# Second half of a hybrid attention and hyena layer on one core: low parts of three projections on VectorE, the first merge chunk by token halves, the loads of the second modulation from GpSimd's queue

## The chip, the cores and the metric

The kernel runs on one core of one Trainium2 chip. The metric is the device time of one launch in microseconds. The core's engines are TensorE (PE: matrix products and transposes), VectorE (DVE), ScalarE (ACT), GpSimd (POOL) and SyncE (SP). Each of them works its instructions off in their order. A DMA is started by the engine in whose order its issue stands; before the change nearly all of them stand on SP. TensorE's clock is granted at one of two levels, 1.2 and 2.4 GHz, and the profile shows the granted share of the full one.

## What is computed

One layer over 1024 tokens of width 1024: two token mixers side by side, attention (8 heads) and a hyena long convolution (512 channels), each projected to the model's width, gated, added, and passed through one output projection with a gated residual. A norm with a second modulation and a feed-forward net follow. What bears on the change:

```python
m = silu(c) @ w_mod + b_mod                     # six modulation vectors of 1024
# modulation 2, 3 and 4, 5: the second half, "w_mod2" in the kernel
y  = sigmoid(g_attn) * (attn @ w_attn_out) + sigmoid(g_hyena) * (hyena @ w_hyena_out)
x  = x + gate1 * (y @ w_o + b_o)
h2 = rmsnorm(x, norm2) * (1 + scale2) + shift2  # then the feed-forward net
```

All is float32. The kernel splits each float32 operand of a product into a high part (`hi`, rounded to the shorter float32r) and a low part (`lo` = operand minus `hi`) and adds three products, hi*hi, hi*lo and lo*hi (`mm3`, lines L184 to L186).

## The kernel before

Stages follow one another: attention, then the hyena merge, the attention-branch merge, the output projection `wo`, the feed-forward net. A scheduler puts the instructions of these stages into one fixed order for each engine; tiles come from pools with a fixed number of buffers, and an instruction that needs a buffer waits until its last reader is done.

**Weights.** A block of weights is loaded by SP (`raw`), rounded by ScalarE (`whi`), and the low part `wlo` is made by one subtraction of 128 x 512 (`sub`, L174). `load_w` does this for the merges, `halves_of` for the output projection. In this part of the program that subtraction runs on GpSimd (`G`), except for the first hyena chunk, which has it on VectorE.

**Hyena merge** (L1242 on). The hyena output is stored by tokens and turned by TensorE into `hyh` and `hyl` (high and low part), four z tiles of which two make up each half of 512 tokens; a z tile gives two channel blocks, each by four transposes into a PSUM tile `tr` (2 buffers), a cast on ScalarE and a subtraction on VectorE. All four z tiles come first in the program, then four chunks `ci` of two output blocks `m2`. `branch` computes one output block over both token halves into a PSUM tile `mm` (3 buffers): per half 4 k steps of three matmuls. The result is multiplied by the sigmoid of `sg` (loaded by SP, sigmoid on ScalarE) and stored as `th_d`. In all 192 matmuls of 512 columns.

**Attention-branch merge** (L1262 on). The same with 8 k steps, on the attention output `oTh`, `oTl`; to its product the stored `th` is added, and the sum is split into `m0h`, `m0l` (first token half) and `m1h`, `m1l`. 384 matmuls. The last piece of the attention output is made by GpSimd (`ou`, `oTl`) and ScalarE (`oTh`).

**Output projection** (`wo_part`, `wo_get`). Four parts (token half, column half), each of 8 k steps over 4 row tiles, 384 matmuls in all. `wo_get` keeps five blocks of `w_o` loaded and three split ahead. At the end of a part VectorE evacuates each PSUM tile: `tm` (times the gate row), `Yt` plus `tm`, and in the first column half `Yt` plus the bias row `brow`. Beside the second token half, the first half is normed and turned (`first_rows`, `first_tile`: transposes L1391, `hf`, `m0h`, `m0l`); for odd blocks the low part `m0l` is on GpSimd.

**The second modulation** (`mod2`) runs beside all three stages, one step of four loads at each `background(1)`: for each of 8 blocks (j, n), 8 loads of 256 KB of `w_mod2` into `wm` (3 buffers), each multiplied by its part of silu(c) and added into `acc` by VectorE (L1209, L180). When four loads of the next block are done, `row_out` adds up `acc` over the partitions (high part `ah` on ScalarE, low part `al` on VectorE, two matmuls with a column of ones into `tr`), loads the row of `b_mod2`, adds it on VectorE (`row`), and stores the row in `m2_d`. All these transfers are SP's (`ld` is SP's issue of a DMA).

The functions that the change touches, with what calls them:

Of the kernel before, what the change touches and what calls it, by code (L numbers as in the profile page):

```python
# [15 lines left out]
P = 128  # L16
# [149 lines left out]
def build(tc, A, out, stop=99):  # L166
# [1018 lines left out]
    def row_out():  # L1185
# [9 lines left out]
        row = mp.tile([1, 512], F32, name="row", tag="row", bufs=2)  # L1195
        ld(out=row, in_=A["b_mod2"][j:j + 1, 512 * n:512 * n + 512])
        tt(row, row, ps[0:1], ALU.add)
        ld(out=m2_d[j:j + 1, 512 * n:512 * n + 512], in_=row)

    def mod2():  # L1200

        for j in (2, 0, 1, 3):
            for n in range(2):
                acc = mp.tile([P, 512], F32, name="acc", tag="acc", bufs=2)
                for k in range(KT):
                    raw = mp.tile([P, 512], F32, name="wm", tag="wm", bufs=3)
                    ld(out=raw, in_=A["w_mod2"][j, k][:, 512 * n:512 * n + 512])
                    if k == 0:
# [13 lines left out]
    hyl = [z.tile([P, 4, 512], F32R, name="hyl") for z in (zp_, zp2)]  # L1222
    for j, (half, a4) in enumerate(ZT):
        zt = zts[j] if j < 3 else z_load(half, a4)
        for c2 in range(2):
            c = 2 * half + c2
            tp = ptr.tile([P, 512], F32, name="tr", tag="tr")
            for a in range(4):
                T.transpose(tp[:, a * P:a * P + P], zt[:, a, c2 * P:c2 * P + P], ident)
            S.copy(out=hyh[a4][:, c], in_=tp)  # L1230
            sub(hyl[a4][:, c], tp, hyh[a4][:, c])

    def branch(w, m2, kt, rh, rl):
        ps = pmm.tile([P, L], F32, name="mm", tag="mm")
        for h in range(2):
            cs = slice(512 * h, 512 * h + 512)
# [6 lines left out]
    for ci in range(4):  # L1243
        w = load_w(A["w_hy"][ci], wp, G, nraw=5) if ci else load_w([raw_hy[:, 0], raw_hy[:, 1]], wp, V, nraw=5)
        for m2 in range(2):
            m = 2 * ci + m2
            ps = branch(w, m2, 4, hyh, hyl)
            sg = sgp.tile([P, L], F32, name="sg", tag="sg")
# [13 lines left out]
    for ci in range(4):  # L1262
        w = load_w(A["w_attn"][ci], wp, G, nraw=5)
        for m2 in range(2):
# [64 lines left out]
    def wo_get(half, n, k):  # L1329
# [4 lines left out]
        for b_ in wo_blocks[i:i + 3]:  # L1334
            if b_ not in wo_ready:
                wo_ready[b_] = halves_of(wo_raw_[b_], G)
        return wo_ready[half, n, k]
# [71 lines left out]
    def first_tile(c):  # L1409
        h2_tile(0, c, ptr.tile([P, 512], F32, name="tr", tag="tr"), hf0[:, c], S if c % 2 else V)  # L1410
        to_parts([b_[:, c] for b_ in B1], hf0[:, c], G if c % 2 else V)

# [462 lines left out]
```

## Time and profile before

| | |
|---|---|
| time, median of 3 runs | 1963.72 us (1960.64 to 1965.02) |
| profiled execution | 1968.5 us, span 1966.8 us |
| mean granted clock of TensorE | 0.979 |
| TensorE, VectorE busy | 1883.7 us (96%), 1548.1 us (79%) |
| ScalarE, GpSimd busy | 968.0 us (49%), 200.6 us (10%) |
| hyena merge | 1051.0 to 1103.5 us |
| attention-branch merge | 1103.5 to 1193.2 us |
| output projection | 1193.2 to 1297.6 us |
| DMA queues | SP 287.01 MB, ScalarE 33.76 MB, GpSimd none |

A program orders the rows by engine: "busy" is the time in which an engine executes, "idle before" the time in which it stood before an instruction, with the instruction or DMA that released it. The times are those of one profiled execution, counted from its span's start; the span is 1.7 us shorter than the time of that execution.

### The profile page before, as it was taken

The numbers are of one execution on the slowest core, as the hardware profiler recorded it, in microseconds if no ns is written. First come the engines' busy times: TensorE is split into PE (matmuls) and PEld (weight loads), VectorE is DVE, ScalarE is ACT, GpSimd is POOL, SyncE is SP. The second block draws the span as 40 slices with busy tenths as digits, with TensorE's granted clock in tenths as the row PEclk, the third lists the DMA queues.
The fourth block names the chain that finished last, engine by engine and source line by source line (L and its number), as shares of the span: only waits on it lengthen the run. The fifth ranks groups of instructions, "written<-read, shape, count | busy, mean of one in ns | idle before, by whom it ended". The sixth has DMA issues, their size and how long they took to land.

```text
span 1966.8 us, 27637 instructions
## 1 busy us (share of the span) xinstructions
PE 1883.7 (96%) x9776; PEld 1567.7 (80%) x9776; DVE 1548.1 (79%) x2753; ACT 968.0 (49%) x1958; POOL 200.6 (10%) x147
## 2 busy tenths in 40 slices
PE   7899999999999999999998999999999999899997
PEld 1788788999898987888887787778888888678885
DVE  6999996895978764777776555988888888878787
ACT  3855553432534365777775232454444444445443
POOL 0000000000000002445412233510000000000000
PEclk8999999999999999999999999999999999999998
DMA  8517437756554433544408865632323333358762
GB/s 297 181 57 249 133 135 237 220 177 196 185 169 148 156 136 102 151 136 143 145 17 216 297 215 209 214 113 86 118 97 123 102 113 107 124 182 320 252 204 96
DMA packets 181130, 322.53 MB, mean 164 GB/s; under 512 B 26955, under 2 KB 65359, under 8 KB 180096
## 3 DMA queue, kind: packets, MB, share of 16 engines
q1 hardware_dynamic: 156256, 287.01, 44.8%
q10 hardware_dynamic: 24736, 33.76, 4.8%
q8 instruction: 77, 1.26, 0.3%
q14 instruction: 61, 0.50, 0.1%
HBM read 245.03 MB, written 75.68 MB: 163 GB/s over the span
## 4 chain that ended last, share of the span: by engine, by line
PE 64%; DVE 19%; issue 5%; DMA 4%; ACT 3%; POOL 0%; SPq 0%; ACTq 0%; DVEq 0%; POOLq 0%
PE mm L184 8%; PE mm L185 8%; PE mm L186 8%; PE b L184 5%; PE b L186 5%; PE b L185 5%; PE tp L1145 3%; DVE ua L180 2%; DVE ug L180 2%; PE s L184 2%; PE s L186 2%; PE s L185 2%; PE o L185 2%; PE o L186 2%; PE o L184 2%
## 5 line engine op out<-in xcount | busy, mean ns | idle before, releaser
L184 PE MATMUL mm<-hTh,whi 128*128 128x512 f32 x448 | 177.8, 397 | 3.1 <-ACT sg L974 1.4
L185 PE MATMUL mm<-hTl,whi 128*128 128x512 f32 x448 | 177.1, 396 | 0.0
L186 PE MATMUL mm<-hTh,wlo 128*128 128x512 f32 x448 | 176.0, 393 | 0.0
L1047 DVE TENSOR_REDUCE mx<-s 128x1 f32<-128x512 f32 (+1 forms) x192 | 113.4, 598 | 55.3 <-PE s L186 53.6
L174 DVE TENSOR_TENSOR wlo<-raw,whi 128x512 fp32r<-128x512 f32 x158 | 106.6, 688 | 45.4 <-ACT whi L1513 32.1
L1052 ACT ACTIVATE Pt<-s,mx 128x512 f32<-128x512 f32 (+1 forms) x192 | 116.2, 616 | 18.4 <-DVE mx L1050 17.0
L184 PE MATMUL mm<-whi,hTh 128*128 128x256 f32 x416 | 119.6, 289 | 4.2 <-ACT whi L497 3.2
L174 DVE TENSOR_TENSOR PTl<-tp,PTh 128x512 fp32r<-128x512 f32 x160 | 108.4, 685 | 14.7 <-ACT PTh L1147 11.2
L185 PE MATMUL mm<-wlo,hTh 128*128 128x256 f32 x416 | 119.8, 289 | 0.0
L186 PE MATMUL mm<-whi,hTl 128*128 128x256 f32 x416 | 119.6, 288 | 0.0
L1147 ACT CAST PTh<-tp 128x512 fp32r<-128x512 f32 x160 | 92.9, 594 | 40.5 <-PE tp L1145 40.5
L186 PE MATMUL b<-bh,al 128*128 128x512 f32 x284 | 110.6, 389 | 0.6 <-DVE al L174 0.6
L184 PE MATMUL b<-bh,ah 128*128 128x512 f32 x284 | 110.6, 389 | 0.3 <-ACT ah L1732 0.3
L185 PE MATMUL b<-bl,ah 128*128 128x512 f32 x284 | 110.6, 389 | 0.0
L497 ACT CAST whi<-raw 128x512 fp32r<-128x512 f32 x110 | 67.1, 618 | 79.6 <-PE mm L185 37.7
L388 ACT CAST Xh<-X 128x512 fp32r<-128x512 f32 x128 | 77.8, 620 | 51.5 <-DVE X L177 18.9
L184 PEld LDWEIGHTS mm<-hTh,whi 128*128 128x128 f32 x448 | 84.7, 189 | 19.2 <-ACT sg L974 1.8
L174 DVE TENSOR_TENSOR Xl<-X,Xh 128x512 fp32r<-128x512 f32 x128 | 85.1, 682 | 18.1 <-ACT Xh L388 17.6
L174 POOL TENSOR_TENSOR qT<-qf,qT 128x1024 fp32r<-128x1024 f32 x7 | 16.7, 2393 | 801.5 <-ACT qT L1019 801.5
L186 PEld LDWEIGHTS mm<-hTh,wlo 128*128 128x128 f32 x448 | 84.5, 189 | 15.5 <-DVE wlo L174 0.2
L174 POOL TENSOR_TENSOR wlo<-raw,whi 128x512 fp32r<-128x512 f32 x54 | 80.0, 1493 | 161.6 <-ACT whi L497 103.1
L1145 PEld LDWEIGHTS tp<-ident,Pt 128*128 128x128 f32 x640 | 78.0, 141 | 22.7 <-issue 3.8
(385 smaller groups left out, 5761.1 us busy)
## 6 DMA issues: line engine op xcount, KB each, us to landing
raw<-w_up SPq DMA_DIRECT2D x132, 256.0 KB, 2.8
raw<-w_in SPq DMA_DIRECT2D x88, 256.0 KB, 4.3
wm<-w_mod SPq DMA_DIRECT2D x64, 256.0 KB, 4.2
raw<-act_d SPq DMA_DIRECT2D x25, 512.0 KB, 3.2
wd<-w_down SPq DMA_DIRECT2D x44, 256.0 KB, 3.6
ws_d<-wd SPq DMA_DIRECT2D x44, 256.0 KB, 4.4
act_d<-ug SPq DMA_DIRECT2D x44, 256.0 KB, 2.2
ft<-fwd_d SPq DMA_DIRECT2D x28, 384.0 KB, 3.7
```

The source lines that it names most:

```text
L174: eng.tensor_tensor(out=out, in0=a, in1=b, op=ALU.subtract)
L180: eng.scalar_tensor_tensor(out=out, in0=a, scalar=s, in1=b, op0=op0, op1=op1)
L184: T.matmul(o, lh, rh, start=start, stop=False, skip_group_check=more)
L185: T.matmul(o, lh, rl, start=False, stop=False, skip_group_check=more)
L186: last_mm[0] = T.matmul(o, ll, rh, start=False, stop=stop, skip_group_check=more)
L388: S.copy(out=h, in_=X)
L497: S.copy(out=hi, in_=raw)
L1047: V.tensor_reduce(out=mx[:, j:j + 1], in_=s[:, :n], axis=AX.X, op=ALU.max)
L1052: S.activation(out=Pt[:, o:o + n], in_=sps[j][:, :n], func=AF.Exp, bias=mx[:, 3:4], accum_out=sm[:, j:j + 1])
L1145: T.transpose(tp[:, i * P:i * P + P], cur[i][:, kt * P:kt * P + P], ident)
L1147: S.copy(out=th, in_=tp)
```

## The change

Three edits, all between the end of attention and the end of the output projection. First, the low parts of the hyena weights of chunks 1 to 3 (6 subtractions), of the attention-branch weights (16) and of `w_o` (32), and the four odd `m0l` of `first_tile`, move from GpSimd to VectorE. Second, the z tiles become a function: the first chunk of the hyena merge transposes the two z tiles of the first token half, multiplies that half for both output blocks, then transposes the other two z tiles and multiplies the second half into the same PSUM tiles. Third, the loads of `wm`, of the `b_mod2` rows and the stores of `m2_d` are issued from GpSimd's queue (`G.dma_start`) instead of SP's. GpSimd has no other work left in these stages after its last `ou` and `oTl`.

```diff
@@ row_out, mod2
-        ld(out=row, in_=A["b_mod2"][j:j + 1, 512 * n:512 * n + 512])
+        G.dma_start(out=row, in_=A["b_mod2"][j:j + 1, 512 * n:512 * n + 512])
         tt(row, row, ps[0:1], ALU.add)
-        ld(out=m2_d[j:j + 1, 512 * n:512 * n + 512], in_=row)
+        G.dma_start(out=m2_d[j:j + 1, 512 * n:512 * n + 512], in_=row)
...
-                    ld(out=raw, in_=A["w_mod2"][j, k][:, 512 * n:512 * n + 512])
+                    G.dma_start(out=raw, in_=A["w_mod2"][j, k][:, 512 * n:512 * n + 512])
@@ hyena merge
-    for j, (half, a4) in enumerate(ZT):
+    def z_tile(j):
+        half, a4 = ZT[j]
...
-    def branch(w, m2, kt, rh, rl):
-        ps = pmm.tile([P, L], F32, name="mm", tag="mm")
-        for h in range(2):
+    def branch(w, m2, kt, rh, rl, hs=(0, 1), ps=None):
+        ps = pmm.tile([P, L], F32, name="mm", tag="mm") if ps is None else ps
+        for h in hs:
...
-        w = load_w(A["w_hy"][ci], wp, G, nraw=5) if ci else load_w([raw_hy[:, 0], raw_hy[:, 1]], wp, V, nraw=5)
+        w = load_w(A["w_hy"][ci], wp, nraw=5) if ci else load_w([raw_hy[:, 0], raw_hy[:, 1]], wp, nraw=5)
+        if ci == 0:
+            z_tile(0)
+            z_tile(1)
+            first = [branch(w, m2, 4, hyh, hyl, (0,)) for m2 in range(2)]
+            z_tile(2)
+            z_tile(3)
         for m2 in range(2):
...
-            ps = branch(w, m2, 4, hyh, hyl)
+            ps = branch(w, m2, 4, hyh, hyl, (1,), first[m2]) if ci == 0 else branch(w, m2, 4, hyh, hyl)
@@ attention-branch merge
-        w = load_w(A["w_attn"][ci], wp, G, nraw=5)
+        w = load_w(A["w_attn"][ci], wp, nraw=5)
@@ output projection, first_tile
-                wo_ready[b_] = halves_of(wo_raw_[b_], G)
+                wo_ready[b_] = halves_of(wo_raw_[b_])
...
-        to_parts([b_[:, c] for b_ in B1], hf0[:, c], G if c % 2 else V)
+        to_parts([b_[:, c] for b_ in B1], hf0[:, c])
```

What the scheduler makes of it is shown at three places, all in VectorE's order. The first is the start of the hyena merge: `hyl` of `hyh0` is of the first token half, of `hyh1` of the second; `acc` is an accumulation of the second modulation. Before:

```order
L174 TENSOR_TENSOR hyl_12221<-tr_12244,hyh0_12219 128x512
L174 TENSOR_TENSOR hyl_12222<-tr_12251,hyh1_12220 128x512
L1209 TENSOR_SCALAR acc_12319<-wm_12320,sc_178 128x512
L174 TENSOR_TENSOR hyl_12222<-tr_12258,hyh1_12220 128x512
L174 TENSOR_TENSOR hyl_12222<-tr_12267,hyh1_12220 128x512
L180 SCALAR_TENSOR_TENSOR acc_12319<-wm_12323,sc_178,acc_12319 128x512
```

After:

```order
L174 TENSOR_TENSOR hyl_12221<-tr_12252,hyh0_12219 128x512
L1209 TENSOR_SCALAR acc_12332<-wm_12333,sc_178 128x512
L180 SCALAR_TENSOR_TENSOR acc_12332<-wm_12336,sc_178,acc_12332 128x512
L180 SCALAR_TENSOR_TENSOR acc_12332<-wm_12339,sc_178,acc_12332 128x512
L180 SCALAR_TENSOR_TENSOR acc_12332<-wm_12342,sc_178,acc_12332 128x512
L174 TENSOR_TENSOR hyl_12222<-tr_12285,hyh1_12220 128x512
L174 TENSOR_TENSOR hyl_12222<-tr_12292,hyh1_12220 128x512
```

Four accumulations now stand ahead of the second half's first `hyl`, where one stood between its first and second.

The second place is VectorE's order around the first result of the attention-branch merge (`sg_12744`). `wlo_12844` and `wlo_12850` are the low parts of chunk 1 for k 4 to 7, which stood on GpSimd before. Before, with 24 accumulations ahead of the first row:

```order
L177 TENSOR_TENSOR sg_12744<-mm_12695,sg_12744 128x1024
L1209 TENSOR_SCALAR acc_12815<-wm_12816,sc_178 128x512
L177 TENSOR_TENSOR sg_12744<-sg_12744,th_12747 128x1024
L180 SCALAR_TENSOR_TENSOR acc_12815<-wm_12819,sc_178,acc_12815 128x512
L174 TENSOR_TENSOR m0l_12668<-sg_12744,m0h_12667 128x512
```

After, with 39 ahead of it:

```order
L177 TENSOR_TENSOR sg_12744<-mm_12695,sg_12744 128x1024
L180 SCALAR_TENSOR_TENSOR acc_13079<-wm_13172,sc_178,acc_13079 128x512
L177 TENSOR_TENSOR sg_12744<-sg_12744,th_12747 128x1024
L174 TENSOR_TENSOR m0l_12668<-sg_12744,m0h_12667 128x512
L174 TENSOR_TENSOR m1l_12670<-sg_12744,m1h_12669 128x512
L174 TENSOR_TENSOR wlo_12844<-raw_12840,whi_12842 128x512
L174 TENSOR_TENSOR wlo_12850<-raw_12846,whi_12848 128x512
```

The accumulations have moved ahead by two blocks, and the two low parts stand behind the last of them and behind the first result.

The third place is VectorE's order at the first evacuation of the output projection (`tm_13544`, `Yt`), where `acc_13429` is the sixth block. `wlo_13494` and `wlo_13512` are k 6 and 7 of the first part, `wlo_13530` to `wlo_13592` k 0 to 3 of the second. Before:

```order
L1209 TENSOR_SCALAR acc_13429<-wm_13430,sc_178 128x512
L177 TENSOR_TENSOR tm_13544<-w_13373,brow_13360 128x512
L180 SCALAR_TENSOR_TENSOR acc_13429<-wm_13433,sc_178,acc_13429 128x512
L177 TENSOR_TENSOR Yt_13344<-Yt_13344,tm_13544 128x512
L180 SCALAR_TENSOR_TENSOR acc_13429<-wm_13436,sc_178,acc_13429 128x512
L177 TENSOR_TENSOR Yt_13344<-Yt_13344,brow_13362 128x1024
```

After (the eight accumulations of `acc_13429` and the low parts of k 6, 7, 0 and 1 stand ahead of these rows):

```order
L1209 TENSOR_SCALAR acc_13647<-wm_13648,sc_178 128x512
L174 TENSOR_TENSOR al_13621<-acc_13429,ah_13619 128x512
L180 SCALAR_TENSOR_TENSOR acc_13647<-wm_13651,sc_178,acc_13647 128x512
L180 SCALAR_TENSOR_TENSOR acc_13647<-wm_13654,sc_178,acc_13647 128x512
L177 TENSOR_TENSOR tm_13544<-w_13373,brow_13360 128x512
L174 TENSOR_TENSOR wlo_13586<-raw_13526,whi_13584 128x512
L177 TENSOR_TENSOR Yt_13344<-Yt_13344,tm_13544 128x512
```

The first evacuation stood behind one accumulation of this stage and stands behind eleven; `wlo_13592` follows after all four tiles' `tm` and `Yt`.

## Rows read from the trace of the kernel before

**Rows 1.** The page's busy times, and its two groups of low-part subtractions
```profile
PE 1883.7 (96%) x9776; PEld 1567.7 (80%) x9776; DVE 1548.1 (79%) x2753; ACT 968.0 (49%) x1958; POOL 200.6 (10%) x147
...
L174 DVE TENSOR_TENSOR wlo<-raw,whi 128x512 fp32r<-128x512 f32 x158 | 106.6, 688 | 45.4 <-ACT whi L1513 32.1
...
L174 POOL TENSOR_TENSOR wlo<-raw,whi 128x512 fp32r<-128x512 f32 x54 | 80.0, 1493 | 161.6 <-ACT whi L497 103.1
```

**Rows 2.** Stretches: us; PE, PEld, DVE, ACT, POOL busy; clock, DMA, GB/s
```profile
1050.99:1103.50 52.51, 49.12 (x220) 39.83 (x221) 32.83 (x39) 17.84 (x24) 8.97 (x7) 0.97 0.83 282
1103.50:1193.20 89.70, 88.84 (x390) 72.34 (x389) 48.35 (x54) 28.16 (x43) 25.44 (x18) 1.00 0.63 213
1193.20:1297.60 104.40, 97.31 (x425) 77.86 (x423) 82.96 (x95) 36.30 (x60) 48.50 (x32) 0.97 0.65 218
1195.27:1219.80 24.53, 24.53 (x108) 20.29 (x109) 10.56 (x11) 5.50 (x9) 10.50 (x7) 1.00 0.89 329
```

**Rows 3.** Hyena start, timeline: start, length (us), operation, [idle before <-releaser]
```profile
1054.20 1.26 POOL L177 TENSOR_TENSOR ou<-ou,rb 128x512 f32<-128x512 f32 x1 [9.57 <-DMA rb<-rd_d]
1055.49 0.62 ACT L1096 CAST oTh<-ou 128x512 fp32r<-128x512 f32 x1 [4.07 <-POOL ou L177]
1056.02 1.07 ACT L1230 CAST hyh<-tr 128x512 fp32r<-128x512 f32 x2
1056.19 1.27 POOL L1097 TENSOR_TENSOR oTl<-ou,oTh 128x512 fp32r<-128x512 f32 x1 [0.73 <-ACT oTh L1096]
...
1057.38 0.66 PE L1229 MATMUL tr<-ident,zt 128*128 128x128 f32 x4 [3.38 <-DVE hyl L174]
...
1059.30 0.48 DVE L1209 TENSOR_SCALAR acc<-wm,sc 128x512 f32<-128x512 f32 x1
```

**Rows 4.** Timeline of TensorE in attention chunk 0, and at chunk 1's start
```profile
1109.58 0.50 PE L186 MATMUL mm<-oTh,wlo 128*128 128x512 f32 x1 [0.61 <-POOL wlo L174]
...
1126.05 0.39 PE L186 MATMUL mm<-oTh,wlo 128*128 128x512 f32 x1
1126.28 0.39 PE L184 MATMUL mm<-oTh,whi 128*128 128x512 f32 x1
```

**Rows 5.** Timeline of the output projection: TensorE, and ScalarE before its longest gap
```profile
1195.27 0.50 PE L184 MATMUL w<-whi,m0h 128*128 128x512 f32 x1 [1.43 <-DVE row L177]
...
1227.16 0.62 ACT L1314 CAST whi<-raw 128x512 fp32r<-128x512 f32 x1 [5.97 <-DMA raw<-w_o]
...
1228.35 0.39 PE L1193 MATMUL tr<-ah,ones 128*1 128x512 f32 x1 [3.10 <-ACT ah L1189]
...
1229.31 0.63 PE L186 MATMUL w<-whi,m0l 128*128 128x512 f32 x1
...
1259.72 0.48 PE L1391 MATMUL tr<-ident,Yt 128*128 128x128 f32 x1 [0.99 <-DVE Yt L1386]
```

**Rows 6.** VectorE from 1195 to 1297.6: count, busy us, mean ns, idle before
```profile
L180 DVE SCALAR_TENSOR_TENSOR acc<-wm,sc,acc 128x512 f32<-128x512 f32 x21 | 24.1, 1147 | 2.9 <-DMA wm<-w_mod 2.7
L177 DVE TENSOR_TENSOR Yt<-Yt,brow 128x1024 f32<-128x1024 f32 x8 | 13.7, 1706 | 0.0
L177 DVE TENSOR_TENSOR Yt<-Yt,tm 128x512 f32<-128x512 f32 x15 | 12.7, 853 | 0.2
L177 DVE TENSOR_TENSOR tm<-w,brow 128x512 f32<-128x512 f32 x15 | 10.1, 681 | 3.3 <-PE w L186 3.3
```

**Rows 7.** Tile wm: ns minimum/median/maximum, first and last start; landing
```profile
L1207 SPq DMA_DIRECT2D wm<-w_mod x64: 327/328/1008, 1049.8 to 1260.9; - x64
L180 DVE SCALAR_TENSOR_TENSOR acc<-wm,sc,acc x56: 732/752/1878, 1062.9 to 1264.8; 128x512 f32<-128x512 f32 x56
...
DMA to landing us min/median/max: 2.7/4.3/7.0
```

**Rows 8.** SP from 1020 to 1330, waits: us, times, longest us
```profile
SPq L1309 <- POOL wlo L174: 47.1, 20, 14.7
SPq L1207 <- DVE acc L180: 31.2, 28, 3.0
```

## The prediction

> **What bounds the kernel now.** I read the busy times first: TensorE is busy 96% of the span, VectorE 79%, GpSimd 10% [rows 1]. So only time in which TensorE stands, or runs at its low clock, can be won, and only in the stages that the change touches. The second view gives these stages by stretch [rows 2]: in the hyena merge TensorE lacks 52.51 - 49.12 = 3.4 us, in the attention-branch merge 89.70 - 88.84 = 0.9, in the output projection 104.40 - 97.31 = 7.1. The granted clock is 0.97, 1.00 and 0.97 there; 3% of the first and third stretch are 1.6 and 3.1 us more, spent at 1.2 instead of 2.4 GHz. In all 3.4 + 0.9 + 7.1 + 1.6 + 3.1 = 16 us, 0.8% of the time, is the most that the change could give.
>
> The third view, the timeline around each gap, says what ended it. Hyena: the gap of 3.38 us is a chain, the row of softmax sums landing at 1054.2, GpSimd's last ou, ScalarE's cast of it, and only then the casts of hyh that stand behind it on ScalarE [rows 3]. Attention chunk 0: 0.61 us for a low part made by GpSimd [rows 4]. Output projection: 1.43 us at the entrance for VectorE's row add, 3.10 us at 1228.35, nominally for ah, but ScalarE had just before waited 5.97 us for a w_o block, with ah queued behind that cast, and 0.99 us (the longest of four) for VectorE's Yt; a matmul behind the 3.10 us gap takes 0.63 us against 0.39 elsewhere, which is the low clock [rows 4, 5]. SP spent 31 us in wm loads waiting for a buffer that VectorE had to release, and 47 us in weight loads waiting for GpSimd's low parts [rows 8]: one queue carries both, so a wait of either holds the other.
>
> **Low parts to VectorE.** 54 low parts leave GpSimd at 1.493 us and arrive at VectorE at 0.688 us [rows 1]; with four m0l of the same shape, 58 x 0.688 = 39.9 us more work on VectorE. Where this matters is the output projection: 32 of GpSimd's instructions lie in it [rows 2], so 32 x 0.688 = 22.0 us come to VectorE's 82.96. Against that, VectorE is slow there while GpSimd works: an accumulation takes 1.147 us in this stretch, 0.752 in the median over the kernel and 1.878 at worst [rows 6, 7]; if GpSimd's arithmetic is the reason, 21 x (1.147 - 0.752) = 8.3 us come back. Yt<-Yt,tm at 0.853 against 0.681 for tm, of the same size: 15 x 0.172 = 2.6. Yt<-Yt,brow is twice as long, so at most 2 x 0.681 clean: 8 x (1.706 - 1.362) = 2.8. Sum 82.96 + 22.0 - 13.7 = 91 us, of some 98 that TensorE needs. VectorE keeps up, with 7 us to spare; each us that it waits for a wm load beyond that moves the end.
>
> In the hyena and attention merges 22 low parts come to VectorE, 22 x 0.688 = 15 us of 142, where it is busy 33 and 48 us: hidden, but for one place. The three that now stand inside attention are worth between 0 and 3 x 0.688 = 2.1 us; I take 0.
>
> The place is chunk 1 of the attention merge. By the order its low parts for k 4 to 7 stand on VectorE behind all 40 accumulations of five wm blocks (24 before), and TensorE wants the first of them 14 matmuls after chunk 1 starts at about 1126.8: at the pace of 1126.28 - 1126.05 = 0.23 us [rows 4] that is 1130.0. The accumulations start at about 1061 (the first load cannot be issued before oTl ends at 1056.19 + 1.27 [rows 3], and takes 2.7 to 4.3 us). Three buffers go round: a load is asked for when VectorE has released one, lands L later and is used for 0.752 us, so they come every (L + 0.75) / 3. No load of before was issued by GpSimd; the nearest row is SP's own, 2.7, 4.3 and 7.0 us to landing (minimum, median, maximum) [rows 7]. With L = 4.5 (the median and the wait for the queue) the cadence is 1.75 us, the 40th lands at 1061 + 37 x 1.75 = 1125.8; behind it stand an add, two halves of m0l, m1l and the low part, 1.2 + 1.4 + 0.7 = 3.3 us, so 1129.1: in time. Each us more of L costs 37 / 3 = 12.3 us here. I take 1.5 us; bounds 0 (L at 2.7) and 12 (L at 5.5); at 7.0 it would be 30, but 7.0 is the worst load of 64, not a mean.
>
> **The token halves.** The first half's 48 matmuls need only the first two z tiles. That does not move the first gap: ScalarE's order there, two casts, oTh, two casts, is the same. The gap shrinks by 0 to 0.7, as the matmuls no longer wait for the transposes in front. A new gap may open: the second half's third transposition needs a hyl that now stands behind four accumulations. TensorE comes there after 26 matmuls and two transpositions: 9 at the low clock's pace (about 0.43, twice the 0.23) and 17 at 0.23 from 1056.6, 1056.6 + 3.9 + 3.9 + 0.9 = 1065.3. The fourth load waits for the first buffer, freed at 1060.7 to 1062.3, and two row loads stand before it on GpSimd's queue at, if as on SP, 0.33 us each [rows 7]: it lands at 1064 to 1067, and the hyl is out by 1065.4 to 1068.7. So 0.1 to 3.4 us, at a slow load 5; I take 1.5. With the 0.7 that the first gap gives: +0.8 (bounds -0.7 and +5).
>
> **The loads on GpSimd's queue.** 64 wm loads, 8 row loads and 8 stores leave SP, 80 x 0.33 = 26 us of issue, and GpSimd, with no arithmetic left in this stretch, has time for them: 10 per cent busy before [rows 1]. What SP gains is that w_attn, w_o, sg and th loads no longer stand behind a wm load that waits for VectorE [rows 8]. That removes the 0.61 us in chunk 0 (-0.6; bounds 0 and -0.6), and the late w_o cast that made the 3.10 us gap. What it costs: a store waits for VectorE's row add, and the wm loads of the next block stand behind it on GpSimd. Three loads are in flight ahead, so a wait below one cadence costs nothing; above that up to 1.75 us for each of the three or four stores ahead of the 40th load, which belongs to the 12 above.
>
> The Trainium skill, "DMA: Bandwidth & Descriptors", § Specifications, gives the first byte of a DMA from GpSimd at about 1 us and from SP at about 0.6. No run so far shows a load from GpSimd here. By that, as an estimate, L would be 0.4 longer and the place in chunk 1 some 5 us worse, the time about 1966.
>
> **Output projection.** The entrance gap (1.43) stays: VectorE's row add and the transfers to the new PSUM tiles are the same. The gap of 3.10 goes, with its low clock: 8 matmuls at 0.43 instead of 0.23, 1.6 us; together -4.7. The four gaps at Yt had VectorE's slow accumulations before them: -1.0. In their place: the first evacuation of PSUM (tm) now stands on VectorE behind 11 more accumulations, and the low part of k 3 of the next part behind all twelve evacuation steps. The evacuation is due at about 1213, the loads are there by 1195 + 8 x 1.75 + 1 = 1210; but this stretch is the fullest of all for the DMA engines, share 0.89 at 329 GB/s [rows 2]. I take +1.7 for them, so -4.0 for the stage. Bounds: -8.8 (7.1 - 1.43 of gaps and 3.1 of clock all gone) and +4 (loads of 7 us: 8 x 2.6 instead of 8 x 1.75, 6.6 late, less the 2.7 of slack, on top of nothing won).
>
> **Sum.** +0.8 (hyena) - 0.6 (chunk 0) + 1.5 (chunk 1) - 4.0 (projection) = -2.3 us. The profiled run took 1968.5 us with a span of 1966.8 and lies 4.8 us above the median of 1963.72; the difference goes on the median: 1961.4, say 1961.
>
> **The rivals.** (1) All comes free: loads come in 3.5 us, neither new gap opens, VectorE without GpSimd beside it has every low part early. -0.7 - 0.6 - 8.8 = -10 at most; with one small gap left -8, 1956. For it: GpSimd's queue is empty otherwise, and the wm loads need not stand behind 512 KB transfers. Against it: the same bytes in the fullest stretches.
> (2) Slower, the pacing of VectorE by wm loads: accumulations and low parts are now in one in-order engine, and a late load holds the low part behind it. It decides at chunk 1, and from L = 4.6 upwards. At L = 5.5 the cadence is 2.08, the 40th lands at 1138, 3.3 behind it, against 1130: +11.3; hyena +2.5; chunk 0 -0.6; the projection gives only -2. +11, 1975.
> (3) The change doesn't free VectorE: the slow accumulations come from GpSimd's use of memory, and issuing loads is GpSimd's work too. Then the 13.7 us don't come back, and VectorE has 105 us to do where TensorE has 98: +7 for that, +1.7 for the rest, 1972. No row of before can tell it, since GpSimd issued nothing. The Trainium skill, "SBUF — State Buffer", § SBUF: two separate sides, warns of it from the other end: a load issued from GpSimd is held up while VectorE runs certain copy-like operations, and the page's advice is to issue from SP or ScalarE, which speaks against this part of the change. Only 8 of the 64 accumulations are tensor_scalar, the kind that it names; by it, case 2 would be likelier than case 1.
>
> **How the numbers follow.** The forecast with its neighbourhood, 1957 to 1967: 0.42. Case 1: 0.25. Case 2: 0.23. Case 3: 0.10. A measurement of this kernel tells some 0.2%, 3.9 us, from no change. The forecast's own case lies 0.13 below 1959.8 and 0.29 above; so faster 0.13 + 0.25 = 0.38, same 0.29, slower 0.33. The range for 8 in 10 reaches from case 1's end, 1953, to case 2's, 1975.
>
> **What would show it.** Of each step: the four m0l and 54 low parts at about 0.69 us on VectorE and accumulations in the projection near 0.75 (otherwise case 3); the wm loads' time to landing and the distance between accumulations, 1.75 us; VectorE's wait for wm just before the low parts of chunk 1, and TensorE's gap there; a gap of up to 3 us at the second half's third transposition; no gap at the row matmul in the projection, and SP's waits in wm loads gone. Wrong it would be above all if L is not near 4.5 us.

## The result and the profile after

The changed kernel takes 1985.16 us (median of 4 runs, 1983.97 to 1986.75) where the kernel before takes 1964.12: ratio 1.0117, interval 1.0099 to 1.0134. It is 21 us slower; 1961 was forecast, with 1975 as the upper end. The profile's busy times after, beside [rows 1]:

```profile
PE 1885.6 (95%) x9776; PEld 1567.2 (79%) x9776; DVE 1556.0 (78%) x2811; ACT 966.5 (49%) x1958; POOL 158.1 (8%) x169
```

TensorE's work is the same; the span grew by 18 us in the profiled runs. The stretches of the three stages, cut at their first matmuls, first of the kernel before and then of the changed one (us; busy times of PE, PEld, DVE, ACT, POOL; granted clock, DMA share, GB/s):

```profile
1050.99:1103.72 52.73, 49.34 (x220) 40.02 (x221) 32.83 (x39) 17.84 (x24) 8.97 (x7) 0.97 0.83 282
1103.72:1195.27 91.55, 89.26 (x392) 72.24 (x390) 50.21 (x57) 28.78 (x44) 27.37 (x19) 1.00 0.63 212
1195.27:1297.60 102.33, 96.68 (x422) 77.77 (x422) 81.10 (x93) 35.68 (x59) 46.58 (x30) 0.97 0.65 218
...
1049.33:1106.17 56.84, 48.85 (x220) 38.38 (x220) 32.46 (x46) 17.21 (x24) 18.72 (x32) 1.00 0.82 284
1106.17:1208.21 102.04, 92.66 (x390) 74.80 (x390) 56.15 (x74) 28.70 (x44) 10.05 (x19) 0.95 0.54 176
1208.21:1315.20 106.99, 98.54 (x421) 78.89 (x422) 80.94 (x124) 35.66 (x59) 16.68 (x31) 0.95 0.61 207
```

The hyena merge takes 4.1 us more, the attention merge 10.5, the projection 4.7: 19.3 us. In the last two the granted clock is 0.95, where it was 1.00 and 0.97: of the 10.5 us, 3.4 are TensorE's longer busy time (92.66 against 89.26) and 7.1 are idle time. Outside the three stages the span before has 1720.2 us, the changed one 1719.1.

VectorE's groups in the projection answer to [rows 6] (count, busy us, mean ns, idle before):

```profile
L174 DVE TENSOR_TENSOR wlo<-raw,whi 128x512 fp32r<-128x512 f32 x30 | 20.2, 681 | 3.2 <-ACT whi L1321 2.0 <-ACT whi L1520 1.2
L180 DVE SCALAR_TENSOR_TENSOR acc<-wm,sc,acc 128x512 f32<-128x512 f32 x21 | 15.7, 747 | 15.0 <-DMA wm<-w_mod 15.0
...
L177 DVE TENSOR_TENSOR Yt<-Yt,brow 128x1024 f32<-128x1024 f32 x8 | 9.7, 1213 | 0.0
L177 DVE TENSOR_TENSOR Yt<-Yt,tm 128x512 f32<-128x512 f32 x14 | 9.5, 684 | 0.1
```

An accumulation takes 0.747 us instead of 1.147, Yt<-Yt,brow 1.213 instead of 1.706, Yt<-Yt,tm 0.684 instead of 0.853: the first edit does what it says. But VectorE stood 15 us before accumulations in this stage. Its waits over all three stages (us, times, longest), and the tile wm as in [rows 7]:

```profile
DVE acc L180 <- DMA wm<-w_mod: 44.7, 34, 3.1
...
DVE sg L177 <- PE mm L186: 6.8, 3, 5.0
...
DVE acc L1209 <- DMA wm<-w_mod: 5.1, 4, 3.0
```

```profile
L1207 POOL DMA_DIRECT2D wm<-w_mod x64: 536/536/729, 1054.0 to 1265.5; - x64
L180 DVE SCALAR_TENSOR_TENSOR acc<-wm,sc,acc x56: 732/751/754, 1058.2 to 1271.9; 128x512 f32<-128x512 f32 x56
...
DMA to landing us min/median/max: 2.8/4.7/8.2
```

Before, its waits for wm loads came to 21.6 us over the kernel; here 49.8, over 38 times. The issue of a load takes 0.54 us instead of 0.33. The landing line is of the 64 loads of the second modulation alone. The line in [rows 7], 2.7/4.3/7.0, is thinner than it looks: it also takes in the first modulation's loads at the kernel's start, and the profile tells the landing of only 9 of SP's 64 loads of the second modulation, 2.7/4.2/7.0. On GpSimd's queue it tells all 64.

Where the waits reach TensorE, the timeline shows (start, length, operation, idle before and its releaser). First the second half's transposes in the hyena merge, where the forecast saw a gap of 0.1 to 3.4 us:

```profile
1061.56 0.75 DVE L180 SCALAR_TENSOR_TENSOR acc<-wm,sc,acc 128x512 f32<-128x512 f32 x1 [1.86 <-DMA wm<-w_mod]
1062.23 1.28 DVE L174 TENSOR_TENSOR hyl<-tr,hyh 128x512 fp32r<-128x512 f32 x2
...
1062.96 0.66 PE L1230 MATMUL tr<-ident,zt 128*128 128x128 f32 x4 [2.11 <-DVE hyl L174]
```

Then two gaps that the forecast did not have, at the end of the hyena merge:

```profile
1095.33 0.75 DVE L180 SCALAR_TENSOR_TENSOR acc<-wm,sc,acc 128x512 f32<-128x512 f32 x1 [2.80 <-DMA wm<-w_mod]
1095.99 1.22 DVE L177 TENSOR_TENSOR sg<-mm,sg 128x1024 f32<-128x1024 f32 x1
...
1097.27 0.50 PE L184 MATMUL mm<-hyh,whi 128*128 128x512 f32 x1 [2.06 <-DVE sg L177]
...
1104.23 0.75 DVE L180 SCALAR_TENSOR_TENSOR acc<-wm,sc,acc 128x512 f32<-128x512 f32 x1 [3.12 <-DMA wm<-w_mod]
1104.90 1.22 DVE L177 TENSOR_TENSOR sg<-mm,sg 128x1024 f32<-128x1024 f32 x1
...
1106.17 0.50 PE L184 MATMUL mm<-oTh,whi 128*128 128x512 f32 x1 [2.71 <-DVE sg L177]
...
1108.10 0.63 PE L184 MATMUL mm<-oTh,whi 128*128 128x512 f32 x1
```

A gate product (sg<-mm,sg) is what empties a PSUM tile. It is ready to run, but stands on VectorE behind an accumulation that waited 2.8 and 3.1 us for its load; with three PSUM tiles, TensorE then has none to write. Behind the second gap the clock falls to its low level for a while (0.63 us for a matmul at 1108.10). Third, chunk 1 of the attention merge:

```profile
1136.89 0.75 DVE L180 SCALAR_TENSOR_TENSOR acc<-wm,sc,acc 128x512 f32<-128x512 f32 x1 [0.32 <-DMA wm<-w_mod]
1137.56 1.22 DVE L177 TENSOR_TENSOR sg<-sg,th 128x1024 f32<-128x1024 f32 x1
...
1138.81 0.62 ACT L1284 CAST m0h<-sg 128x512 fp32r<-128x512 f32 x1 [5.68 <-DVE sg L177]
...
1139.46 0.69 DVE L174 TENSOR_TENSOR m0l<-sg,m0h 128x512 fp32r<-128x512 f32 x1 [0.68 <-ACT m0h L1284]
1139.85 1.13 ACT L497 CAST whi<-raw 128x512 fp32r<-128x512 f32 x2
1140.07 0.68 DVE L174 TENSOR_TENSOR m1l<-sg,m1h 128x512 fp32r<-128x512 f32 x1
...
1140.52 0.79 PE L184 MATMUL mm<-oTh,whi 128*128 128x512 f32 x1 [7.94 <-ACT whi L497]
1140.67 1.28 DVE L174 TENSOR_TENSOR wlo<-raw,whi 128x512 fp32r<-128x512 f32 x2
```

The 40th accumulation ends at 1137.6; behind it the sum, ScalarE's m0h and m1h, and only behind these the cast of the weights: 7.94 us of gap, and the first matmul behind it runs at the low clock (0.79 us). The chain of waits before it consists for the most part of wm loads and GpSimd's queue; some of its steps (start, length, step):

```profile
1107.08 5.42 DMA wm<-w_mod
...
1122.93 0.50 POOL m_d L1198
...
1128.28 0.50 POOL row L1196
...
1128.78 4.06 DMA wm<-w_mod
```

Two gaps that the forecast set out to remove are gone: the 0.61 us in chunk 0 and the 3.10 us at the row matmul. But in the projection two evacuations are late in the same way as the gate products, 3.9 and 2.4 us:

```profile
1236.93 0.80 PE L184 MATMUL w<-whi,m0h 128*128 128x512 f32 x1 [3.90 <-DVE tm L177]
```

```profile
1264.57 0.80 PE L184 MATMUL w<-whi,m1h 128*128 128x512 f32 x1 [2.44 <-DVE tm L177]
```

### The profile page after: what moved, and what is told of

It reads as the page before. It is cut to its first block, busy times and chain, and to the rows that moved or that the text cites. A ratio compares the mean times of both kernels' runs of the same rounds, so it can differ in the third digit from the quotient of the medians.

```text
span 1985.0 us, 27667 instructions
## 1 busy us (share of the span) xinstructions
PE 1885.6 (95%) x9776; PEld 1567.2 (79%) x9776; DVE 1556.0 (78%) x2811; ACT 966.5 (49%) x1958; POOL 158.1 (8%) x169
## 4 chain that ended last, share of the span: by engine, by line
PE 59%; DVE 19%; DMA 9%; issue 5%; ACT 3%; POOL 0%; SPq 0%; ACTq 0%; DVEq 0%; POOLq 0%
PE mm L184 7%; PE mm L185 7%; PE mm L186 7%; PE b L184 6%; PE b L186 6%; PE b L185 6%; DMA wm<-w_mod 4%; PE tp L1145 3%; PE s L184 2%; PE s L186 2%; PE s L185 2%; PE o L185 2%; DVE ua L180 2%; PE o L186 2%; PE o L184 2%
## 5 line engine op out<-in xcount | busy, mean ns | idle before, releaser
L174 DVE TENSOR_TENSOR wlo<-raw,whi 128x512 fp32r<-128x512 f32 x212 | 143.0, 687 | 68.2 <-ACT whi L1520 32.6
L1145 PE MATMUL tp<-ident,Pt 128*128 128x128 f32 x640 | 94.9, 275 | 1.7 <-DVE PTl L174 1.4
L185 PEld LDWEIGHTS mm<-hTl,whi 128*128 128x128 f32 x448 | 84.7, 189 | 14.4
```

The costliest lines, as they stand in the source:

```text
L174: eng.tensor_tensor(out=out, in0=a, in1=b, op=ALU.subtract)
L185: T.matmul(o, lh, rl, start=False, stop=False, skip_group_check=more)
L1145: T.transpose(tp[:, i * P:i * P + P], cur[i][:, kt * P:kt * P + P], ident)
```

## The experiments

Theories: **order** (with the loads on GpSimd's queue the schedule places accumulations far ahead on VectorE, 40 instead of 24 before chunk 1's low parts, and what TensorE needs waits behind them); **queue** (loads from GpSimd's queue are late in themselves); **VectorE** (40 us of low parts are too much for it). The start of the hyena merge lies between 1040.2 and 1051.3 us in the profiled runs, from differences that exist before the changed stages; so stage lengths tell more than totals. They are cut at the first matmul of each stage and at the last of the projection, each in one profiled execution. Two kernels that agree in a stage can still differ there: e10 and e14 have the same numbers of accumulations ahead of the gate products in the merges, and 95.9 and 93.4 us in the attention merge. Ratios and differences from "before" go by the kernel before as it was measured beside each (medians of 1961.85 to 1964.12 us):

| kernel | median us | ratio to before (interval) | hyena | attention | projection |
|---|---|---|---|---|---|
| before | 1964.12 | | 52.7 | 91.5 | 102.3 |
| changed | 1985.16 | 1.0117 (1.0099 to 1.0134) | 56.8 | 102.0 | 107.0 |
| e1 lows, halves, SP | 1958.56 | 0.9980 (0.9969 to 0.9991) | 48.1 | 92.2 | 98.3 |
| e2 only the queue | 1996.94 | 1.0180 (1.0158 to 1.0201) | 60.8 | 108.5 | 113.4 |
| e3 only the lows | 1954.78 | 0.9964 (0.9948 to 0.9979) | 51.6 | 90.7 | 97.4 |
| e8 only the halves | 1960.32 | 0.9991 (0.9973 to 1.0009) | 50.2 | 93.1 | 101.7 |
| e5 changed, rows on SP | 1985.75 | 1.0106 (1.0081 to 1.0130) | 58.4 | 103.6 | 105.2 |
| e6 changed, 4 wm buffers | 1979.77 | 1.0075 (1.0047 to 1.0103) | 54.6 | 101.7 | 105.2 |
| e7 changed, 1 load of 8 | 1949.25 | 0.9928 (0.9900 to 0.9956) | 51.5 | 90.1 | 92.7 |
| e9 order ahead, SP | 1971.03 | 1.0033 (1.0020 to 1.0046) | 51.3 | 101.9 | 99.3 |
| e4 paced, GpSimd | 1976.08 | 1.0073 (1.0051 to 1.0095) | 54.0 | 100.0 | 109.0 |
| e10 paced, SP | 1961.48 | 0.9988 (0.9972 to 1.0005) | 48.6 | 95.9 | 98.1 |
| e13 paced, GpSimd, projection in SP's order | 1973.31 | 1.0053 (1.0034 to 1.0072) | 52.5 | 99.2 | 107.4 |
| e14 paced, SP, projection's order ahead | 1959.52 | 0.9986 (0.9968 to 1.0005) | 49.5 | 93.4 | 97.4 |
| e15 as e13, wm on ScalarE's queue | 1969.44 | 1.0028 (0.9990 to 1.0066) | 51.0 | 99.2 | 103.2 |
| e11 e3 with 4 wm buffers | 1954.48 | 0.9952 (0.9931 to 0.9973) | 49.6 | 90.1 | 98.1 |
| e12 e1 with 4 wm buffers | 1953.14 | 0.9943 (0.9923 to 0.9963) | 49.6 | 91.2 | 96.7 |

**One edit at a time.** e1, the changed kernel with the third edit undone:

```diff
-                    G.dma_start(out=raw, in_=A["w_mod2"][j, k][:, 512 * n:512 * n + 512])
+                    ld(out=raw, in_=A["w_mod2"][j, k][:, 512 * n:512 * n + 512])
```

(and the same for `row` and `m2_d`).

> The changed kernel with the loads, rows and stores of the second modulation back on SP: low parts on VectorE and token halves remain. Theory O (the loss comes from the accumulations that the schedule places far ahead on VectorE once the loads are on GpSimd's queue: each waits for its load, and low parts, gate products and evacuations wait behind it): in this kernel the order has 22 to 24 accumulations ahead of the attention merge's first result again, as before the change, so 1955 to 1965 us, no gap of 8 us at chunk 1, waits for wm on VectorE under 30 us. Rival V (the 40 us of low parts are too much for VectorE): still 1975 to 1985. Rival Q (only the queue's own latency counts): 1955 to 1965 too.

1958.56 us: the third edit costs 26.6 us against this, and as all low parts are on VectorE here too, its load is not the cause. e2, the third edit alone, on the kernel before:

> The kernel before with the third edit alone: loads, rows and stores of the second modulation from GpSimd's queue, low parts still on GpSimd, z tiles first. Theory O: 40 accumulations stand ahead of the attention merge's first result by the order here too, and the low parts now stand on GpSimd behind load issues that wait for buffers: at least as slow as the changed kernel, 1980 to 2000. Rival V: 1960 to 1968, as VectorE has no more to do than before. Rival Q: 1975 to 1985.

1996.94, slower than all three together. The gap at chunk 1 is longer still. It ends, as in the changed kernel, with ScalarE's cast of the weights; GpSimd's next low part waited 8.36 us for a cast of these weights too, so low parts behind load issues, which the expectation names, are not what this gap waited for:

```profile
1144.16 0.79 PE L184 MATMUL mm<-oTh,whi 128*128 128x512 f32 x1 [10.49 <-ACT whi L497]
```

e3, the first edit alone:

> The kernel before with the first edit alone: the 58 low parts on VectorE, loads on SP, z tiles first. Theory O and rival Q: the order of accumulations is as before, so 1957 to 1967; accumulations in the output projection near 0.75 us instead of 1.15. Rival V: 1975 to 1985.

1954.78 against 1963.16 of the kernel before, and a little below the range expected: 8.4 us is what the first edit gains by itself. The projection (columns as above) and the accumulations in it:

```profile
1186.80:1284.20 97.40, 94.28 (x421) 76.72 (x422) 79.64 (x124) 35.60 (x59) 0.00 (x0) 0.98 0.70 228
```

```profile
L180 DVE SCALAR_TENSOR_TENSOR acc<-wm,sc,acc 128x512 f32<-128x512 f32 x21 | 15.6, 741 | 1.4 <-DMA wm<-w_mod 1.4
```

97.4 us instead of 102.3, accumulations at 0.741 us, and 1.4 us of idle time before them where the changed kernel has 15.0. e8, the halves alone (weights' low parts back on GpSimd, loads on SP):

> The kernel before with the token halves alone: low parts on GpSimd, loads on SP. From the difference of the two runs with and without it (1958.56 and 1954.78, intervals just apart) it costs 0 to 4 us: 1962 to 1968. If the halves are worth nothing by themselves: 1960 to 1966. The first gap of TensorE in the hyena merge is about 0.9 to 2.5 us instead of 3.4.

1960.32, its interval includes no change; the hyena merge itself is 2.5 us shorter. TensorE's first gap became 2.1 us.

**What in the loads.** e5, the rows and stores back on SP, the 64 loads on GpSimd's queue:

```diff
-        G.dma_start(out=row, in_=A["b_mod2"][j:j + 1, 512 * n:512 * n + 512])
+        ld(out=row, in_=A["b_mod2"][j:j + 1, 512 * n:512 * n + 512])
```

> The changed kernel with the 8 row loads and 8 row stores back on SP, the 64 wm loads still on GpSimd's queue; VectorE's order around the attention merge is unchanged (39 accumulations ahead of its first result, 40 ahead of chunk 1's low parts). Theory O(a), each load's round trip with three buffers sets the pace: 1981 to 1987, about as the changed kernel. Theory O(b), the stores that wait for VectorE's row add and the row loads that wait for a store hold the wm loads behind them on GpSimd: 1974 to 1980, the gap of 7.9 us at chunk 1 shrinks below 4.

1985.75: no gain. The stores stand in the chain of waits, but without them the chain runs through the next load. e6, four buffers:

```diff
-                    raw = mp.tile([P, 512], F32, name="wm", tag="wm", bufs=3)
+                    raw = mp.tile([P, 512], F32, name="wm", tag="wm", bufs=4)
```

> The changed kernel with four wm buffers instead of three; 40 accumulations still stand ahead of chunk 1's low parts. Theory O(a): a load every (4.9 + 0.75) / 4 = 1.4 us instead of 1.9, so the gaps at chunk 1 and at the gate products go, 1962 to 1975. Theory O(c), the DMA engines have no more bytes per us to give in these stages: the loads take longer to land in the same measure, 1981 to 1988. Theory O(b): 1978 to 1986.

1979.77, 5 us better, less than the 10 to 20 that O(a) gives, more than O(c). It lies in the range given to O(b), which e5 speaks against. The loads took longer in turn, a median of 5.0 us instead of 4.7 (the 4.9 in the expectation takes in the first modulation's loads):

```profile
DMA to landing us min/median/max: 2.9/5.0/9.8
```

e7, one load per block, read by all eight accumulations (seven of eight loads are left out):

```diff
-                for k in range(KT):
-                    raw = mp.tile([P, 512], F32, name="wm", tag="wm", bufs=3)
-                    G.dma_start(out=raw, in_=A["w_mod2"][j, k][:, 512 * n:512 * n + 512])
+                raw = mp.tile([P, 512], F32, name="wm", tag="wm", bufs=3)
+                G.dma_start(out=raw, in_=A["w_mod2"][j, 0][:, 512 * n:512 * n + 512])
+                for k in range(KT):
```

> The changed kernel with one wm load per block of the second modulation instead of eight, read by all eight accumulations: 56 loads of 256 KB and their waits are left out, VectorE's work is all there. Theory O in all its forms: 1945 to 1960, no gap over 2 us between the hyena merge's start and the norm but the entrance of the projection. Rival V (VectorE's added work): 1970 to 1980, as its work is unchanged.

1949.25, and VectorE's idle time for wm (us, times) falls to

```profile
  DMA wm<-w_mod: 6.1, 4
```

So VectorE can do all its work, low parts included, with the projection in 92.7 us. Without the waits, and without the 14.7 MB that e7 also takes off the DMA engines, the changed kernel is 36 us shorter: the loss is in the loads.

**Order against queue.** e4 keeps the queue and holds the order back, by tying each accumulation to the gate product or evacuation ahead of it in the program:

```diff
+                    with tc.issue_after(last_sg[0].ins):
                         if k == 0:
...
-            tt(sg, ps, sg, ALU.mult)
+            last_sg[0] = V.tensor_tensor(out=sg, in0=ps, in1=sg, op=ALU.mult)
```

> The changed kernel with the loads still on GpSimd's queue, but each accumulation ordered on VectorE behind the gate product (in the projection: behind the evacuation) that stands before it in the program, so that 24 instead of 40 stand ahead of chunk 1's low parts of the attention merge, and none ahead of the hyl. Theory O: the gap of 8 us at chunk 1 and the one at the hyl go, 1958 to 1970. Rival Q: the loads stay as late as they are, and hold VectorE as often: 1978 to 1988. Rival V: 1975 to 1985.

1976.08, between the theories. So four more kernels set order and queue apart. e9 has the loads on SP and VectorE's order of the changed kernel in the merges:

```diff
+            background((2, 1, 1, 1, 2, 1, 2, 1)[m])
+            with tc.issue_after(last_acc[0].ins):
+                tt(sg, ps, sg, ALU.mult)
```

> Low parts on VectorE and token halves, loads of the second modulation on SP, but the accumulations written ahead in the program and the gate products ordered behind them, so that VectorE's order in the merges is nearly that of the changed kernel (8, 8, 12, 16, 20, 24, 28, 32 and 40 accumulations ahead of the nine first gate products; changed kernel 8, 9, 11, 15, 19, 23, 27, 31, 39). The projection has the order of the kernel before (40 ahead of its first evacuation). Theory order: the merges take about as long as in the changed kernel, 56.9 and 102.0 us, the projection 97 to 99: 1972 to 1980. Theory queue (loads from GpSimd's queue as such are late): merges near 48 and 92 us, 1955 to 1962.

1971.03, just below the range of the order theory. The attention merge takes 101.9 us, the changed kernel 102.0, e1 92.2: in this pair nearly all of the loss there comes with the order. It is spread otherwise, in gaps of 2.11 us at a gate product and of 2.20 and 3.89 us in chunk 1 instead of one of 7.94; each gate product waits here for up to one accumulation more. The end of chunk 1's chain, with the 40th load from SP:

```profile
1124.62 0.75 DVE L1212 SCALAR_TENSOR_TENSOR acc<-wm,sc,acc 128x512 f32<-128x512 f32 x1 [1.82 <-DMA wm<-w_mod]
1125.29 2.35 DVE L177 TENSOR_TENSOR sg<-mm,sg 128x1024 f32<-128x1024 f32 x2
...
1127.55 2.35 DVE L177 TENSOR_TENSOR sg<-sg,th 128x1024 f32<-128x1024 f32 x2
...
1131.02 0.69 DVE L174 TENSOR_TENSOR wlo<-raw,whi 128x512 fp32r<-128x512 f32 x1
...
1131.76 0.79 PE L186 MATMUL mm<-oTh,wlo 128*128 128x512 f32 x1 [3.89 <-DVE wlo L174]
```

In the hyena merge the order costs 3.3 us (51.3 against 48.1), and GpSimd's queue 5.5 more at nearly the same order (56.8). From the first accumulation to the 40th one comes every 1.86 us here, every 2.04 us in the changed kernel. e10, the paced kernel on SP:

> The paced kernel (each accumulation behind the gate product or evacuation before it in the program) with the loads, rows and stores on SP. Its order in the merges is that of the paced kernel within a few accumulations, in the projection that of the kernel before. Theory order: merges 52 to 54 and 98 to 100 us as in the paced kernel, the projection 97 to 99: 1962 to 1970. Theory queue: merges near 48 and 92 us, 1952 to 1960.

1961.48: the same 5.5 us in the hyena merge (54.0 and 48.6), 4.1 in attention, where the queue thus costs something at this order, and 11 in the projection; there, though, the order differs too. e13 gives the paced GpSimd kernel the projection's order of e10 (the edit below), e14 gives e10 the projection's order of e4, by the first evacuation tied behind the accumulations as the gate products in e9:

```diff
-    wo_part(0, 0, {k: (bgs(1),) for k in (0, 2, 3)})
+    wo_part(0, 0, {})
...
+                    if (half, n) == (0, 0) and i < 3:
+                        background(1)
```

> The paced kernel, loads from GpSimd's queue, with the accumulations of the projection's first part written behind its evacuations: 40, 43, 46 and 48 ahead of the four first evacuations, as in the paced kernel on SP (projection 98.0 us there), where the paced kernel on GpSimd's queue had 48 ahead of all four (109.0). Theory order: the projection takes 97 to 101 us here, 1964 to 1969 in all. Theory queue: 105 to 110 us, 1973 to 1978.

> The paced kernel on SP with the first evacuation of the projection ordered behind 48 accumulations, as in the paced kernel on GpSimd's queue; nothing else changed. Theory order: the projection takes 105 to 110 us as there, 1969 to 1973 in all. Theory queue: 97 to 101 us, 1959 to 1964.

The projection is now measured in all four pairs: on SP 98.1 and 97.4 us, on GpSimd's queue 107.4 and 109.0, at 40 and 48 accumulations ahead of the first evacuation. In the projection the order costs nothing and the queue 9 to 12 us. In e13 VectorE waits 4.0 us for a load just ahead of the chain that norms Yt, and TensorE 5.0 us for its result:

```profile
1258.91 0.75 DVE L180 SCALAR_TENSOR_TENSOR acc<-wm,sc,acc 128x512 f32<-128x512 f32 x1 [4.01 <-DMA wm<-w_mod]
...
1261.66 2.06 DVE L1397 TENSOR_SCALAR Yt<-Yt,rs_r 128x1024 f32<-128x1024 f32 x3
...
1262.45 0.48 PE L1402 MATMUL tr<-ident,Yt 128*128 128x128 f32 x1 [5.03 <-DVE Yt L1397]
```

Time to landing can't be compared: for the projection the profile tells it of 2 of SP's 24 loads in the kernel before (2.7 and 3.4 us, a median of 3.0 that e15's expectation takes as the stage's), and in e10 and e14 of none. What every run has is VectorE's waits for these loads in the projection (us, times, longest), on SP in e10,

```profile
DVE acc L180 <- DMA wm<-w_mod: 1.8, 3, 0.9
```

from GpSimd's queue in e13, where all landings are told (median 4.3, maximum 9.0),

```profile
DVE acc L180 <- DMA wm<-w_mod: 8.5, 5, 4.0
```

and from ScalarE's queue in e15, whose edit is `S.dma_start` for the 64 loads:

> The kernel with the projection's order of the paced SP kernel and the loads of the second modulation from GpSimd's queue, with the 64 wm loads issued from ScalarE's queue instead; rows and stores stay on GpSimd. ScalarE's casts then stand behind load issues that wait for buffers, so the time as such says little (1970 to 1990); what counts is the time from issue to landing in the projection, 3.0 us in the median on SP's queue before the change and 4.3 to 4.9 on GpSimd's. If two queues side by side share the DMA engines and each transfer takes longer for it: 4 to 5 us here too. If it is the making of the transfers on GpSimd: 3 to 3.5 us.

```profile
DVE acc L180 <- DMA wm<-w_mod: 5.9, 4, 3.0
```

In e14, the other kernel on SP, they come to 6.2 us. The projection takes 103.2 us in e15, between SP's 98.1 and GpSimd's 107.4. Landing is told for 11 of the loads there, in the median 3.6 us, between the two expectations, and 8.6 at most. So the loads cost less from ScalarE's queue than from GpSimd's and more than from SP's, in one profiled execution each; whether what is left comes of a second queue beside SP's, the runs don't settle, as ScalarE's loads were also issued at other times and its casts stand behind them.

**A better kernel.** e11 and e12, low parts on VectorE without and with the halves, loads on SP, four wm buffers:

> The first edit alone (low parts on VectorE, loads on SP), with four wm buffers. VectorE waits little for wm there (8 us in 10 waits), so 0 to -4 us against that edit's 1954.8: 1950 to 1956.

> Low parts on VectorE and token halves, loads on SP, with four wm buffers: 0 to -5 us against 1958.6 with three: 1952 to 1959. If the halves as such cost anything, it stays above the run with low parts and four buffers by some 4 us; if not, the two are within 2 us.

1954.48 and 1953.14 us: both beat the kernel before by 0.5%, and the halves cost nothing. (With three buffers e1, with the halves, lies 3.8 us above e3, without; the intervals just overlap.) Stretches of e12, columns as above:

```profile
1044.77:1094.40 49.63, 47.96 (x221) 38.87 (x222) 32.51 (x44) 17.65 (x24) 2.56 (x2) 1.00 0.86 294
1094.40:1185.53 91.13, 89.19 (x391) 72.23 (x389) 56.16 (x75) 28.70 (x44) 0.00 (x0) 1.00 0.63 215
1185.53:1282.30 96.77, 94.11 (x422) 76.76 (x423) 79.61 (x124) 35.72 (x59) 0.00 (x0) 0.98 0.67 229
```

## Why the prediction was wrong

**Bound and first edit: right.** VectorE's operations came back to their clean times as expected, and the edit by itself gave 4.9 us in the projection (e3), where the stage's term was -4.0. VectorE's load was oversized, 91 us forecast, 80.9 measured. More came back than the 13.7 us: the durations of VectorE's operations in the stage, cut at the first matmul, add up to 86.8 us before and 88.4 after, so the added low parts, 21 us, were nearly paid for by operations that became shorter. The forecast also started from the stretch of [rows 2], which begins 2 us earlier, and counted the added operations without overlap: successive operations overlap in the rows, an operation of 0.69 us is followed by the next after 0.60, as m0l, m1l and wlo at chunk 1 are (1139.46, 1140.07, 1140.67), 6.8 us in the stage against 5.1 before. Rival 3, contention that stays, is out: accumulations at 0.747 us with GpSimd issuing loads beside them. The Trainium skill, "SBUF — State Buffer", § SBUF: two separate sides, warns of loads from GpSimd held up by VectorE's copy-like operations. No run isolates that. The page's way out is SP's or ScalarE's queue, and a landing in the projection of 9.0 us from GpSimd's queue (e13) has its like on ScalarE's (8.6, e15), so the warning alone does not explain the late loads.

**Token halves: right in kind.** The first gap went from 3.38 to 0.88 us, more than the 0 to 0.7 given: the row of sums that starts its chain was used 1.4 us after the merge's first matmul (1050.76, 1049.33), before 3.2 after it [rows 3], so part of this is the one execution; e8 has 2.1 us. The new gap at the second half was 2.11, within 0.1 to 3.4. What failed in the hyena merge was that only this one operation was followed behind the accumulations. The gate products stand there too, and they free the PSUM tiles: 2.06 and 2.71 us that no step had.

**Chunk 1: the step that failed.** "I take 1.5 us" stands where 7.94 us of gap came, with a stretch at the low clock behind it. The place was right, and so was the rule in kind: from the first accumulation to the 40th (1057.5 to 1136.9) one came every 2.04 us, and (L + 0.75) / 3 gives that with L = 5.4. L was taken at 4.5. For accumulations 4 to 40 the trace gives in the mean 0.33 us from a buffer's release to the issue, 4.72 to landing, and 0.47 more until VectorE, busy with other work or standing for something else, takes the landed load. So the first two were sized at 4.5 and came to 5.05, and the third was put at nothing.

The size was taken from SP's median, 4.3, which rests on ten loads, and "7.0 is the worst load of 64" is the worst of nine; GpSimd's 64 loads lie a little above these in minimum, median and maximum (2.8, 4.7, 8.2). That is not shown to be the queue's doing: in e8, on SP with eight loads told, the median is 4.9 and the maximum 7.2. Nor is the queue the whole of it: with nearly this order on SP (e9) an accumulation came every 1.86 us, an L of 4.8 by the rule, already above the 4.6 from which chunk 1 loses. Whether it is the added demand, 16 loads ahead of chunk 1, that made them longer, no run shows; the DMA share of the hyena merge is 0.82 against 0.83 before. Last, the path: the forecast followed VectorE's order to the low parts, where TensorE's gap ended with ScalarE's cast of the weights, which stands behind m0h and m1h. The Trainium skill, "DMA: Bandwidth & Descriptors", § Specifications, has 0.4 us more for a first byte from GpSimd than from SP; with SP's medians at 4.2 and 4.9 us and GpSimd's at 4.7, no run here shows it. The prediction weighed that sentence and kept 4.5.

**Projection: wrong in sign.** -4.0 forecast, +4.7 measured. The evacuations were thought to be in time by 1.75 us a load; they came 3.9 and 2.4 us late. The order ahead, which the text blamed, costs nothing there on SP (e14); at the same order the queue costs 9.3 us (e10, e13), and VectorE stood 1.8 and 6.2 us for these loads on SP (e10, e14), 8.5 us for those from GpSimd in e13 and 15.0 in the changed kernel. Why loads from GpSimd's queue come late in this stage stays open.

**Rival 2 was the right one,** in its place and its condition, L above 4.6; its 1975 us missed 10, since it left the projection at -2 and did not have the gate products. That its 11.3 us at chunk 1 lie near the merge's +10.5 is in part luck: the accumulations began 3.5 us before its 1061, and 3.4 of the 10.5 us are matmuls at the low clock, which it did not count. Its chance of 0.23 was too low: what it needed was 0.1 us above the value taken.

The loss against e1, 26.6 us by the medians, can be divided by the stages in the table: to the order 3.3 us (hyena) and 9.7 (attention), e1 to e9; to the queue 5.5 (hyena) and 0.2 (attention), e9 to the changed kernel, and 8.7 (projection), e1 to the changed kernel, where e14 shows the order to cost nothing. That is 27.4 us in the profiled runs. It is one way through the table: at the paced order the queue costs 3 to 7 us in attention (e10 and e14 against e13 and e4), and single executions of a like stage differ by up to 2.5 us, so the smaller terms are not firm.

## What to carry to other kernels

Moving a stream of loads to an idle engine's queue can change where the scheduler places their consumers, here 40 instead of 24 ahead of the same low parts; read the consumer engine's order, and count what else stands behind each such consumer, results that free PSUM above all. Put the load's round trip, over the buffers in flight, against the pace at which that order needs them, and let the unknown queue's bound reach beyond the rows of the known one. Ask of a median from how many loads it is, and of which: the one that set L rested on ten. A change of several edits is worth taking apart: here one edit gives 8 us, one about nothing, and one takes 27.

## What the runs showed of the hardware

A 256 KB load issued from GpSimd cost its queue 0.54 us against 0.33 on SP, and landed after 2.8 to 8.2 us in the changed kernel, all 64 loads; on ScalarE's queue after 2.6 to 8.6 (38 of 64 told, e15), on SP's after 2.7 to 7.2 (9 and 8 of 64 told, the kernel before and e8); that a landing as such is later from GpSimd, these figures don't show. With nearly the same order of their consumers the accumulations came every 2.04 us from GpSimd's queue and every 1.86 us from SP's (e9). GpSimd's load issues left VectorE's accumulations in the projection at their clean length (0.747 us), its arithmetic did not (1.147 on average, over the kernel 1.878 at worst). TensorE's low clock came behind the gaps of 2.44, 2.71, 3.90 and 7.94 us in the changed kernel (0.79 to 0.80 us for the first matmul, after 2.71 us 0.50 for the first and 0.63 from the fifth on), not behind those of 2.06 and 2.11, but in e9 behind one of 2.11 (0.80): the length of a gap alone did not say it.
